# A third pair of k-tiles by seven products in the key and value blocks, and a softmax turned one unit later

## The chip, the cores and the metric

The kernel runs on one core of one Trainium2 chip. The core has a matrix engine (PE in the profile, with its weight loads as PEld), three engines for element work (DVE, which is VectorE; ACT, ScalarE; POOL, GpSimd) and SP, whose queue issues most DMAs. The metric is the device time of one execution in microseconds. Before the change it is 2083.93 us, the median of three runs from 2083.45 to 2084.53.

## The reference

One layer of a streaming encoder on 256 frames of width 2048, in float32: half a SwiGLU block, a mixer (pooling and gated linear attention), cross-attention to 256 memory tokens, half a SwiGLU block again, and a last norm. The change lies in the cross-attention:

```
def mem_cross_attention(h, mem_h, w_q, w_kv, w_o):
    q = (h @ w_q).reshape(b, s, XATTN_HEADS, XATTN_HEAD_DIM)
    kv = (mem_h @ w_kv).reshape(b, mem_h.shape[1], 2, XATTN_HEADS, XATTN_HEAD_DIM)
    k, v = kv[:, :, 0], kv[:, :, 1]
    logits = jnp.einsum('bshd,bmhd->bhsm', q, k).astype(jnp.float32) * (XATTN_HEAD_DIM ** -0.5)
    p = jax.nn.softmax(logits, axis=-1).astype(v.dtype)
    o = jnp.einsum('bhsm,bmhd->bshd', p, v).reshape(b, s, D_MODEL)
    return o @ w_o
```

There are 4 heads of width 512; `w_kv` is 2048 x 4096, keys first, values behind.

## The kernel before

**Split products.** A float32 matrix is kept as a high and a low part in the matrix engine's format, and a product is three matmuls: high by high, high by low, low by high. A weight that is loaded raw is therefore split: ACT casts the high part, DVE subtracts it from the raw tile for the low part.

**Units and blocks.** Weights come in units of 1 MB: 256 rows (a pair of k-tiles, numbered g = 0 to 7) by 1024 columns. A block is eight units that add into the same 256 x 1024 result. `Stream` (L34) emits the units in order. Before it emits unit u's matmuls it emits the splits of the units up to u + 2, and behind each split the load of the unit three further on. `st.op(f, n)` puts a function behind the n-th unit from there. The chains `in_turn` (L257) and `among_weights` (L270) keep the weight splits and some sums in the written order on ACT and DVE; apart from that a planner orders each engine's instructions at compile time, by its own estimates, so that an instruction which is not ready lets a later one pass. At run time each engine works its list in order.

**Plain and seven.** A plain unit (`unit_p`, L556) is 2 k-tiles x 2 token halves x 2 column halves = 8 products, 24 matmuls with 512 columns. A unit of a pair that is named in the block's `Sums` is done by Strassen's scheme in Winograd's form (`unit_s`, L539; `seven`, L493): 7 products, 21 matmuls. For that, DVE and ACT also form sums of the weights (`split_seven`, L471: three additions into a tile `T`, a split of three quarters of the raw tile into `xh` and `xl`, and a split of `T` into `wh` and `wl`), and once for all blocks, sums of the activations (`Sums.make`, L413).

**PSUM.** It is handed out as four tiles of 128 x 1024 (`ptile`, L137; the pool with 4 buffers, L109). A block holds two of them for the products of its plain units from its first unit to its last (`open_whole`), and two more from its first seven unit on (`open_parts`). `combine` (L570) reads these last two out behind the last seven unit, and `join` (L584) adds what it made to the other two at the block's end. Everything else that the matrix engine writes in that time, such as transposes (`rows_turned`, `probs`), `logits` and `values`, takes its tile from the same four.

**Cross-attention.** Keys and values are four blocks in a row: keys of heads 0 and 1, their values, keys of heads 2 and 3, their values. They are called K0, V0, K1 and V1 here. Each had two seven units, g = 0 and g = 4, at the places 3 and 6 of the order (1, 5, 2, 0, 3, 6, 4, 7), places counted from 0. `turn_K` runs behind the first unit of a V block, `logits` (with the softmax) behind its second, `probs`, which transposes the softmax and splits it, behind its third, and `values` behind the first unit of the block that follows. The buffers are tight in one more way: in these blocks `xh` and `xl` come from one group `att` of two buffers, and `T` from the group `sg`, of which `combine` takes one too:

```
KV_HOMES = {"T": [("sg", D, 2)], "xh": [("att", 3 * NB, 2)], "xl": [("att", 3 * NB, 2)]}
```

Of the kernel before, what the change touches and what calls it, by code (L numbers as in the profile page):

```python
# [15 lines left out]
D = 2048  # L16
# [4 lines left out]
NB = 512  # L21
# [78 lines left out]
def build(ctx, tc, I, out):  # L100
    nc = tc.nc
    st = Stream()
# [34 lines left out]
    def ptile(name):  # L137
        return psum.tile([P, 2, NB], F32, tag="ps", name=name)
# [6 lines left out]
    def uid(s):  # L145
        cnt[0] += 1
        return f"{s}{cnt[0]}"
# [42 lines left out]
    xs = main.tile([P, KT, 2, S], F32R, tag="xs", name="xs")  # L190
# [79 lines left out]
    def among_weights(f):  # L270


        scalar, vector = behind_weights(f)
        latest["vector"] = vector
        if scalar is not None:
            latest["scalar"] = scalar
# [7 lines left out]
    def split(hi, lo, src):  # L284
        high = nc.scalar.copy(hi, src)
        return high, nc.vector.tensor_tensor(out=lo, in0=src, in1=f32(hi), op=ALU.subtract)
# [339 lines left out]
    def wload(dst, w, k0, n, n0, cols=NB):  # L626
        nc.sync.dma_start(
            dst, w[k0 * P : (k0 + n) * P, n0 : n0 + cols].rearrange("(k p) n -> p k n", p=P)
        )
# [9 lines left out]
    def wwide(w, n0, k0=0, nk=KT):  # L639

        def src(k):
            def load(raw):
                raw = raw.rearrange("p (k n) -> p k n", n=2 * NB)
                if len(loaded) < 3:
                    for kk in range(2):
                        parts = (0, NB) if not loaded else (0,)
                        for c in parts:
                            n = 2 * NB // len(parts)
                            wload(raw[:, kk : kk + 1, c : c + n], w, k + kk, 1, n0 + c, n)
                else:  # L650
                    wload(raw, w, k, 2, n0, 2 * NB)
                next(first_loads, None)
                loaded.append(1)
            return load
        return [src(k0 + k) for k in range(0, nk, 2)]
# [557 lines left out]
    for b in range(2):  # L1213
        block_b(wblock(w_in, (4 + b) * NB), xs, ev_v(b))
        for i in range(2):
            h = 2 * b + i
# [16 lines left out]
    def homes(of):  # L1233
        return lambda: scope.update(shared={tag: list(of[tag]) for tag in of})
# [7 lines left out]
    def xt(name, shape, dt=F32, tag=None, bufs=1):  # L1242
        t = whole_lines(scope["pool"], shape, dt, tag or name, uid(name), bufs)
        xa[name] = t
        return t
# [36 lines left out]
    w_q, w_kv, w_o = I["xattn_w_q"][0], I["xattn_w_kv"][0], I["xattn_w_o"][0]  # L1282
# [2 lines left out]
    q_sums, Q_ORDER = Sums("ye", xs, (4, 5), True, 2), ((0, 1, 2, 3, 6, 4, 5, 7),  # L1285
                                                        (0, 1, 4, 2, 5, 3, 6, 7))
    Q_SEVENS = ((4,), (4, 5))
    kv_sums, KV_ORDER = Sums("ye", xs, (0, 4), True, 2), (1, 5, 2, 0, 3, 6, 4, 7)
    held = {}

    def ev_Q(b):
# [10 lines left out]
    def turn_K(h):  # L1302
        v = rows_turned(held["K", h])
        K = xa["K", h] = xt("K", [P, 4, 2, M], F32R, tag="kv", bufs=2)
        split(K[:, :, 0, :], K[:, :, 1, :], v)

    def ev_V(b):
        def evict(j, c):
            V = xa["V", 2 * b + j] = xt("V", [P, 2, 2, XHD], F32R, tag="kv", bufs=2)
            split(V[:, :, 0, :], V[:, :, 1, :], c)  # L1310
        return evict

    def logits(h):
        ps = ptile(uid("pl"))
        for t in range(2):
            tok = slice(t * P, (t + 1) * P)
            parts = [(d, a, b) for d in range(4) for a, b in ((0, 0), (0, 1), (1, 0))]
            for i, (d, a, b) in enumerate(parts):
                nc.tensor.matmul(  # L1319
                    ps[:, t, :M], ys[:, 4 * h + d, a, tok], xa["K", h][:, d, b, :],  # L1320
                    start=i == 0, stop=i == 11,
                )
        scale = XHD ** -0.5
        nm, sm = xt("nm", [P, 2], bufs=2), xt("sm", [P, 2], bufs=2)
        nc.vector.tensor_reduce(out=nm, in_=ps[:, :, :M], axis=AX.X, op=ALU.max)
        nc.vector.tensor_scalar_mul(nm, nm, -scale)
        pr = xa["P", h] = xt("P", [P, 2, M], bufs=2)
        for t in range(2):
            nc.scalar.activation(
                pr[:, t, :], ps[:, t, :M], AF.Exp, scale=scale, bias=nm[:, t : t + 1],  # L1330
                accum_out=sm[:, t : t + 1],
            )
        nc.vector.reciprocal(out=sm, in_=sm)
        for t in range(2):
            nc.vector.tensor_scalar_mul(pr[:, t, :], pr[:, t, :], sm[:, t : t + 1])

    def probs(h):
        ps = ptile(uid("pt"))
        for mtile in range(2):
            for t in range(2):  # L1340
                nc.tensor.transpose(
                    ps[:, mtile, t * P : (t + 1) * P], xa["P", h][:, t, mtile * P : (mtile + 1) * P], ident
                )
        if h % 2 == 0:
            xt("PT", [P, D], F32R)
        PT = xa["PT", h] = xa["PT"][:, h % 2 * 4 * S : (h % 2 + 1) * 4 * S].rearrange(
            "p (m a s) -> p m a s", m=2, a=2
        )
        split(PT[:, :, 0, :], PT[:, :, 1, :], ps[:, :, :S])

    def values(h):
        for p in range(2):
            ps = ptile(uid("pv"))
            for d in range(2):
                col = slice((2 * p + d) * P, (2 * p + d + 1) * P)
                parts = [(m, a, b) for m in range(2) for a, b in ((0, 0), (0, 1), (1, 0))]
                for i, (m, a, b) in enumerate(parts):
                    nc.tensor.matmul(  # L1358
                        ps[:, d, :S], xa["V", h][:, m, a, col], xa["PT", h][:, m, b, :],
                        start=i == 0, stop=i == 5,  # L1360
                    )
            split_pair(ys, 4 * h + 2 * p, ps[:, :, :S])
# [8 lines left out]
            for c, after in enumerate((5, 7, 6, 9)):  # L1371
                st.op(lambda c=c: mem_fold(c), after)
    st.op(homes(KV_HOMES))
    for g, after in zip(kv_sums.pairs, (0, 2)):
        st.op(lambda g=g: among_weights(lambda: kv_sums.make(g)), after)
    for b in range(2):
        block_s(wwide(w_kv, b * 2 * NB), xs, kv_sums, KV_ORDER, lambda j, c, b=b: held.__setitem__(
            ("K", 2 * b + j), c))
        for j in (1, 0):
            h = 2 * b + j  # L1380
            st.op(lambda h=h: turn_K(h), 1)
        for h in (2 * b, 2 * b + 1):
            st.op(lambda h=h: logits(h), 2)
            st.op(lambda h=h: probs(h), 3)
        block_s(wwide(w_kv, D + b * 2 * NB), xs, kv_sums, KV_ORDER, ev_V(b))
        for h in (2 * b, 2 * b + 1):
            st.op(lambda h=h: values(h), 1)
    st.op(homes(OUT_HOMES))
# [203 lines left out]
def program(shapes):  # L1592
    import concourse.bacc as _bacc

    nc = _bacc.Bacc("TRN2", target_bir_lowering=False, num_devices=1)
    args = {
        name: nc.dram_tensor(f"in_{name}", shapes[name], F32, kind="ExternalInput").ap()
        for name in _INS
    }
    out = nc.dram_tensor("out", _OUT, F32, kind="ExternalOutput").ap()  # L1600
    with tile.TileContext(nc, schedule_with_timeline_sim=True) as tc, ExitStack() as ctx:
        build(ctx, tc, args, out)
    return nc
# [10 lines left out]
```

## Time and profile before

| what | number |
| --- | --- |
| median of the runs | 2083.93 us |
| profiled execution, its whole time | 2082.87 us |
| its span (first to last instruction) | 2081.1 us |
| PE busy | 2069.4 us, 9660 matmuls |
| DVE busy | 1786.8 us |
| ACT busy | 1138.7 us |
| share of the 16 DMA engines in the loads' queue | 61.8% |
| granted clock of the matrix engine | 0.999 |
| block K0 | about 1089.8 to 1134.6 us of the span |
| block V0 | about 1134.6 to 1185.4 us |
| block K1 | about 1185.4 to 1233.3 us |
| block V1 | about 1233.3 to 1284.0 us |

In the profile's rows, L362 are the matmuls of `products`, so plain units; L507 those of `seven`. Where a short instruction of one kind stands amid another, the planner has interleaved units. A row of the timeline has the start in us, the duration in us, the engine, the line and the operation, the tile written and the tiles read, and in square brackets the engine's idle time ahead and what ended it. A mean duration of a matmul is longer than its share of the engine's time, since matmuls overlap: the pace is read from long runs of them. The program splits the weights of a plain unit at L1572 (ACT) and L453 (DVE); those of a seven unit at L486 (sums), L279 and L280 (`xh`, `xl`), L489 and L453 (`T`). On a block's last units POOL takes 768 of the 2048 columns of L453 (L457).

### The profile page before, as it was taken

To read this page: it belongs to the slowest core of one execution; us is meant where nothing else is said; L and a number is where in the kernel's file an instruction comes from. 1 tells how busy PE (TensorE), PEld (TensorE's weight loads), DVE (VectorE), ACT (ScalarE), POOL (GpSimd) and SP (SyncE) were. 2 spreads that over 40 slices of the span, in tenths; PEclk is the share of its full clock that TensorE was granted. 3 is DMA by queue.
4 is the path that set the end of the run, shared out by engine and by line. 5 is a ranking of instruction groups with operands and counts; after the bars stand their busy time and mean duration, and the time that the engine had idled before them with its cause. 6 is when DMAs were issued, how large, how long until landed. Compare 5 with 4: busy or idle time off the path is not lost.

```text
span 2081.1 us, 24346 instructions
## 1 busy us (share of the span) xinstructions
PE 2069.4 (99%) x9660; PEld 1727.4 (83%) x9660; DVE 1786.8 (86%) x1670; ACT 1138.7 (55%) x1128; POOL 98.4 (5%) x87
## 2 busy tenths in 40 slices
PE   9999999999999999999999999999999999999998
PEld 7888888888888888888888888888888888888886
DVE  7998899989998677679788777879988999889987
ACT  7655455644654545455755444656554555545554
POOL 0000000000000000000000000000100010000001
PEclk9999999999999999999999999999999999999999
DMA  7666666566656755557655455666576665676664
GB/s 264 208 199 228 234 223 220 184 222 240 225 200 218 249 166 182 162 185 272 227 179 189 161 182 181 204 222 204 181 243 215 234 209 191 224 242 222 211 226 150
DMA packets 131322, 435.95 MB, mean 209 GB/s; under 512 B 9860, under 2 KB 13544, under 8 KB 130824
## 3 DMA queue, kind: packets, MB, share of 16 engines
q1 hardware_dynamic: 131176, 434.38, 61.8%
q8 instruction: 76, 1.25, 0.2%
q14 instruction: 38, 0.31, 0.0%
q10 hardware_dynamic: 32, 0.01, 0.0%
HBM read 417.58 MB, written 16.78 MB: 209 GB/s over the span
## 4 chain that ended last, share of the span: by engine, by line
PE 99%; DMA 0%; DVE 0%; ACT 0%; SPq 0%; DVEq 0%; issue 0%; ACTq 0%
PE pt L362 59%; PE pt L507 27%; PE pa L347 7%; PE pb L362 2%; PE ph L780 1%; PE pl L1319 1%; PE pv L1358 1%; PE px L791 1%; PE pp L1012 0%; PE pe L362 0%; DMA x<-in_x 0%; PE pa L1039 0%; PE po L1161 0%; PE tm L1267 0%; PE px L717 0%; PE pq L1148 0%
## 5 line engine op out<-in xcount | busy, mean ns | idle before, releaser
L362 PE MATMUL pt<-wh,xs 128*128 128x512 f32 x2128 | 682.4, 390 | 0.3 <-ACT xs L236 0.3
L453 DVE TENSOR_TENSOR wl<-raw,wh 128x2048 fp32r<-128x2048 f32 (+1 forms) x256 | 552.3, 2163 | 141.5 <-ACT wh L1572 141.1
L1572 ACT CAST wh<-raw 128x2048 fp32r<-128x2048 f32 x256 | 489.4, 1913 | 299.9 <-PE pt L362 138.4
L362 PEld LDWEIGHTS pt<-wh,xs 128*128 128x128 f32 x2128 | 398.7, 188 | 82.1 <-ACT xs L236 0.6
L362 PE MATMUL pt<-wh,ys 128*128 128x512 f32 x1472 | 463.8, 389 | 0.0
L489 ACT CAST wh<-T 128x1024 fp32r<-128x1024 f32 x236 | 248.1, 1055 | 363.8 <-DVE T L486 355.4
L362 PE MATMUL pt<-wl,xs 128*128 128x512 f32 x1064 | 414.6, 390 | 0.0
L362 PEld LDWEIGHTS pt<-wh,ys 128*128 128x128 f32 x1472 | 276.2, 188 | 56.9
L362 PE MATMUL pt<-wl,ys 128*128 128x512 f32 x736 | 286.8, 390 | 0.0
L453 DVE TENSOR_TENSOR wl<-T,wh 128x2048 fp32r<-128x2048 f32 (+1 forms) x118 | 264.8, 2244 | 0.8 <-ACT wh L489 0.4
L362 PEld LDWEIGHTS pt<-wl,xs 128*128 128x128 f32 x1064 | 199.8, 188 | 41.0 <-DVE wl L280 0.2
L280 DVE TENSOR_TENSOR xl<-raw,xh 128x1536 fp32r<-128x1536 f32 x118 | 206.7, 1752 | 18.9 <-ACT xh L279 18.9
L279 ACT CAST xh<-raw 128x1536 fp32r<-128x1536 f32 x118 | 174.6, 1479 | 45.1 <-PE pt L507 36.3
L486 DVE TENSOR_TENSOR T<-T,raw 128x512 f32<-128x512 f32 x236 | 163.0, 691 | 6.2
L362 PEld LDWEIGHTS pt<-wl,ys 128*128 128x128 f32 x736 | 138.2, 188 | 28.5
L486 DVE TENSOR_TENSOR T<-raw 128x1024 f32<-128x1024 f32 x118 | 143.9, 1220 | 0.5
L507 PE MATMUL pt<-wh,xs 128*128 128x512 f32 x364 | 141.8, 390 | 0.0
L457 POOL TENSOR_TENSOR wl<-raw,wh 128x768 fp32r<-128x768 f32 x40 | 74.0, 1851 | 1376.2 <-DVE wl L453 1351.4
L507 PE MATMUL pt<-xh,xs 128*128 128x512 f32 x364 | 135.8, 389 | 0.0
L347 PE MATMUL pa<-xs,wh 128*128 128x512 f32 x384 | 135.6, 397 | 0.0
L507 PE MATMUL pt<-wh,xe 128*128 128x512 f32 x320 | 124.3, 389 | 0.0
L347 PE MATMUL pa<-xs,wl 128*128 128x256 f32 x384 | 106.8, 282 | 0.0
(248 smaller groups left out, 2312.2 us busy)
## 6 DMA issues: line engine op xcount, KB each, us to landing
raw<-in_ffn_w_down SPq DMA_DIRECT2D x88, 1024.0 KB, 5.5
raw<-in_ffn_w_up SPq DMA_DIRECT2D x80, 1024.0 KB, 5.0
raw<-in_ffn_w_gate SPq DMA_DIRECT2D x77, 1024.0 KB, 5.1
raw<-in_w_in SPq DMA_DIRECT2D x32, 1024.0 KB, 5.2
raw<-in_xattn_w_kv SPq DMA_DIRECT2D x32, 1024.0 KB, 5.0
raw<-in_w_out SPq DMA_DIRECT2D x16, 1024.0 KB, 5.6
raw<-in_xattn_w_q SPq DMA_DIRECT2D x16, 1024.0 KB, 5.5
raw<-in_xattn_w_o SPq DMA_DIRECT2D x16, 1024.0 KB, 5.6
```

Source lines behind the costliest of these rows:

```text
L279: in_turn("scalar", lambda: nc.scalar.copy(hi, src))
L280: in_turn("vector", lambda: nc.vector.tensor_tensor(out=lo, in0=src, in1=f32(hi), op=ALU.subtract))
L347: nc.tensor.matmul(o, w, x, start=k == 0 and i == 0, stop=last and i == 1)
L362: nc.tensor.matmul(ps, a, w, start=first and i == 0, stop=last and i == 2)
L453: in_turn("vector", lambda: nc.vector.tensor_tensor(out=lo[:, :n], in0=src[:, :n], in1=f32(hi[:, :n]), op=ALU.subtract))
L457: rest = nc.gpsimd.tensor_tensor(out=lo[:, n:], in0=src[:, n:], in1=f32(hi[:, n:]), op=ALU.subtract)
L486: in_turn("vector", lambda: nc.vector.tensor_tensor(out=o, in0=a, in1=b, op=ALU.add))
L489: in_turn("scalar", lambda: nc.scalar.copy(th[:, c], t[:, c]))
L507: nc.tensor.matmul(banks[n], x, w, start=n in fresh and j == 0, stop=n in ends and j == 2)
L780: nc.tensor.transpose(v[:, i, h * P : (h + 1) * P], g[:, h, i * P : (i + 1) * P], ident)
L791: nc.tensor.transpose(v[:, j, h * P : (h + 1) * P], x[:, h, j * P : (j + 1) * P], ident)
L1572: in_turn("scalar", lambda: nc.scalar.copy(hi, raw))
```

## The change

The key and value blocks take a third pair, g = 2, by seven products. K0 gets an order of its own with the seven units at the places 3, 5 and 6; in V0, K1 and V1 they stand at the places 1, 4 and 6. The activations' sums of the new pair are formed behind the third unit of K0, and the tile that holds such sums grows from two pairs to three. `probs` moves from behind the third unit of a V block to behind its fourth.

```
-    kv_sums, KV_ORDER = Sums("ye", xs, (0, 4), True, 2), (1, 5, 2, 0, 3, 6, 4, 7)
+    kv_sums = Sums("ye", xs, (0, 4, 2), True, 3)
+    KV_ORDER = ((1, 5, 3, 0, 6, 4, 2, 7), (1, 0, 3, 5, 2, 6, 4, 7))
...
-    for g, after in zip(kv_sums.pairs, (0, 2)):
+    for g, after in zip(kv_sums.pairs, (0, 2, 3)):
         st.op(lambda g=g: among_weights(lambda: kv_sums.make(g)), after)
     for b in range(2):
-        block_s(wwide(w_kv, b * 2 * NB), xs, kv_sums, KV_ORDER, lambda j, c, b=b: held.__setitem__(
+        block_s(wwide(w_kv, b * 2 * NB), xs, kv_sums, KV_ORDER[b], lambda j, c, b=b: held.__setitem__(
             ("K", 2 * b + j), c))
...
         for h in (2 * b, 2 * b + 1):
             st.op(lambda h=h: logits(h), 2)
-            st.op(lambda h=h: probs(h), 3)
-        block_s(wwide(w_kv, D + b * 2 * NB), xs, kv_sums, KV_ORDER, ev_V(b))
+            st.op(lambda h=h: probs(h), 4)
+        block_s(wwide(w_kv, D + b * 2 * NB), xs, kv_sums, KV_ORDER[1], ev_V(b))
```

## The prediction

> **What bounds the kernel now.** I read the page first, then the list of waits, then the chain, and last the timelines of the engines between 1060 and 1310 us, where keys and values are computed.
>
> ```profile
> PE 2069.4 (99%) x9660; PEld 1727.4 (83%) x9660; DVE 1786.8 (86%) x1670; ACT 1138.7 (55%) x1128; POOL 98.4 (5%) x87
> PE 99%; DMA 0%; DVE 0%; ACT 0%; SPq 0%; DVEq 0%; issue 0%; ACTq 0%
> 1124.61 4.76 PE pt L507 x21
> 1129.37 10.89 PE pt L362 x48
> 1066.35 0.19 PEld L507 LDWEIGHTS pt<-xl,xs 128*128 128x128 f32 x1 [0.39 <-DVE xl L280]
> 1068.26 0.19 PEld L362 LDWEIGHTS pt<-wh,xs 128*128 128x128 f32 x1 [0.21 <-ACT wh L1572]
> 1068.84 0.19 PEld L507 LDWEIGHTS pt<-wl,xs 128*128 128x128 f32 x1 [0.39 <-DVE wl L453]
> ```
>
> The matrix engine is busy for 99% of the span and carries 99% of the chain that ended last, so the time falls when matmuls go and rises when it has to wait. The next two lines, of the chain, give its pace: 10.89 / 48 = 0.227 us for a matmul of 512 columns, 5.44 us for a plain unit, and 4.76 us for a seven unit. The last three are the only waits of the matrix engine in the whole stretch, 0.99 us, and they lie in the query block, where two seven units with one plain unit between them ran late. In K0, V0, K1 and V1 it waits for nothing. These windows show what room DVE has there (the rows are K0, V0, K1, V1 and, for comparison, a block of the first stage of the last FFN; after the length come busy time and count of PE, PEld, DVE, ACT, POOL):
>
> ```profile
> 1089.80:1134.60 44.80, 44.80 (x211) 37.42 (x210) 39.43 (x45) 25.83 (x27) 2.95 (x2) 1.00 0.56 188
> 1134.60:1185.40 50.80, 50.80 (x260) 43.19 (x260) 36.04 (x35) 24.72 (x26) 3.27 (x3) 1.00 0.49 165
> 1185.40:1233.30 47.90, 47.90 (x235) 40.62 (x234) 34.21 (x28) 22.89 (x19) 3.63 (x3) 1.00 0.52 177
> 1233.30:1284.00 50.70, 50.70 (x259) 43.15 (x259) 36.38 (x36) 23.66 (x25) 3.71 (x3) 1.00 0.49 167
> 1661.80:1702.60 40.80, 40.80 (x182) 33.80 (x181) 39.04 (x30) 24.08 (x21) 2.57 (x2) 1.00 0.63 209
> ```
>
> DVE is 71 to 72% busy in V0, K1 and V1 and 88% in K0; the FFN runs at 96% without a wait. ACT, POOL and the DMAs (0.49 to 0.56 of their time) are far from full.
>
> **The matmuls that go.** Four units, one in each block, drop from 24 to 21 matmuls: 12 x 0.227 = 2.72 us. The Trainium skill ("TensorE: Matmul & The Clock Gate", Back-to-back issue gap) gives N/2.4 + 2.5 ns, so 216 ns for 512 columns, for an isolated stream; by it the saving would be an estimated 2.59 us. The measured 227 ns decides.
>
> **What the sums cost DVE.** Rows of a seven unit, of a plain unit (the fifth), and of the activations' sums:
>
> ```profile
> 1114.50 1.22 DVE L486 TENSOR_TENSOR T<-raw 128x1024 f32<-128x1024 f32 x1
> 1116.30 1.41 DVE L486 TENSOR_TENSOR T<-T,raw 128x512 f32<-128x512 f32 x2
> 1117.63 1.75 DVE L280 TENSOR_TENSOR xl<-raw,xh 128x1536 fp32r<-128x1536 f32 x1
> 1119.30 2.29 DVE L453 TENSOR_TENSOR wl<-T,wh 128x2048 fp32r<-128x2048 f32 x1
> 1121.51 2.29 DVE L453 TENSOR_TENSOR wl<-raw,wh 128x2048 fp32r<-128x2048 f32 x1
> 1106.17 0.68 DVE L424 TENSOR_TENSOR j<-xs 128x512 f32<-128x512 f32 x1
> 1109.88 0.29 DVE L436 TENSOR_TENSOR j<-j 128x128 f32<-128x128 f32 x1
> 1115.63 0.28 DVE L286 TENSOR_TENSOR xs<-j,xs 128x128 fp32r<-128x128 f32 x1
> 1115.84 0.55 DVE L286 TENSOR_TENSOR ye<-j,ye 128x384 fp32r<-128x384 f32 x1
> 1126.63 1.49 DVE L453 TENSOR_TENSOR wl<-raw,wh 128x1280 fp32r<-128x1280 f32 x1 [2.84 <-ACT wh L1572]
> ```
>
> A seven unit costs DVE 1.22 + 1.41 + 1.75 + 2.29 = 6.67 us against 2.29, so 4.38 us more per block. In V0, K1 and V1 this fits (36.38 + 4.38 of some 50 us). The new activations' sums, once in K0, are 0.68 + 4 x 0.29 + 0.28 + 0.55 = 2.67 us. K0's DVE then has 39.43 + 4.38 + 2.67 = 46.5 us of work in 44.1. What covers the missing 2.4 us is its lead: it stood idle for 2.84 us late in K0 because the three weight buffers were full. I take zero for this; without that lead it costs 2.4 us.
>
> In K0 the seven units at the places 5 and 6 touch. `xh` and `xl` share two buffers, so the second unit's cast waits until the first has done its nine products with them, 9 x 0.227 = 2.0 us in; then come the cast, `xl` (1.75) and `wl` (2.29), some 7.6 us in with the cast's 1.48 (row below), while the second unit starts at 4.76. High-part matmuls and the plain unit behind can fill part. I take the nearest row, the query block's 0.99 us; bounds: 0 (all filled) and 1.9 us (nothing reordered). In the other blocks at least one plain unit (5.44 us) lies between, which covers it.
>
> **Where the softmax finds no PSUM.** The blocks' order decides this. Rows around V0 (three of a window table of L507 alone, then the timelines):
>
> ```profile
> 1158.50:1161.00 2.50, 2.24 (x9) 1.53 (x9) 1.00 0.00 0
> 1161.00:1169.00 8.00, 0.21 (x1) 0.00 (x0) 1.00 0.39 132
> 1169.00:1172.20 3.20, 2.88 (x12) 2.25 (x12) 1.00 0.02 5
> 1160.38 0.60 PE L1341 MATMUL pt<-ident,P 128*128 128x128 f32 x4
> 1162.91 0.60 PE L1341 MATMUL pt<-ident,P 128*128 128x128 f32 x4
> 1164.59 1.28 DVE L286 TENSOR_TENSOR PT<-pt,PT 128x512 fp32r<-128x512 f32 x2
> 1169.92 1.48 ACT L279 CAST xh<-raw 128x1536 fp32r<-128x1536 f32 x1 [5.79 <-PE pt L507]
> ```
>
> The first seven unit of V0 does its nine matmuls for the two old PSUM tiles at 1158.5 (the 1 in the second row is its ninth, running over), and the twelve for the two new ones only at 1169, after the softmax transposes (L1341) and their reads at 1164.59. The tiles are handed out in the written order, and a tile promised to the softmax is not lent out. The matrix engine lost nothing, since plain units filled in, but the next `xh` came 5.79 us late.
>
> With the first seven unit at place 1, the order is reversed: it takes the two free tiles behind `turn_K`, and `logits` has to wait until `combine` gives them back at the block's end. The softmax then meets the block's end, where DVE has this to do:
>
> ```profile
> 1180.52 0.69 DVE L575 TENSOR_TENSOR sg<-pt,sg 128x512 f32<-128x512 f32 x1 [1.29 <-ACT sg L574]
> 1181.24 1.23 DVE L576 TENSOR_TENSOR sg<-pt,sg 128x1024 f32<-128x1024 f32 x1
> 1182.51 0.69 DVE L579 TENSOR_TENSOR sg<-pt,sg 128x512 f32<-128x512 f32 x1
> 1183.11 1.49 DVE L453 TENSOR_TENSOR wl<-raw,wh 128x1280 fp32r<-128x1280 f32 x1
> 1184.51 2.35 DVE L589 TENSOR_TENSOR sg<-pt,sg 128x1024 f32<-128x1024 f32 x2
> 1150.57 5.63 PE pl L1319 x47
> 1153.37 0.69 DVE L1325 TENSOR_REDUCE nm<-pl 128x2 f32<-128x512 f32 x1 [1.56 <-PE pl L1319]
> 1154.34 1.28 ACT L1329 ACT_TABLE_LOAD   x1 [4.86 <-DVE nm L1326]
> 1156.45 0.20 ACT L1329 ACTIVATION_READ_ACCUMULATOR P<-pl,nm 128x1 f32 x1
> 1156.89 0.62 DVE L1335 TENSOR_SCALAR P<-P,sm 128x256 f32<-128x256 f32 x2
> ```
>
> Count from the start of `combine`. The matrix engine has the last plain unit until 5.1 and the logits of two heads (5.63 x 48/47 = 5.75 us) until 10.8. After that it can go on only with transposes of a ready softmax, or with the next block, which needs two PSUM tiles. DVE: `combine` until 2.7; then, for K1, the seven unit at place 1, 1.22 + 1.41 + 1.75 + 1.49 = 5.9, until 8.6; the first head's maximum until 9.4; one `join` until 10.6; the other until 11.8. The first head's PSUM tile is read out at about 11.7 (2.3 us behind the maximum, for the table load and the exponentials, 1154.34 to 1156.65). The softmax transposes come first in the written order and take the first two tiles that come free, so the next block gets the third, freed at 11.8; I take 12.3, as the scaling of the first head (0.62) stands among the joins on DVE: **V0 to K1 costs 1.5 us**. Bounds: 0, if the planner hands the block an earlier tile; 4.3, if it puts the second head's transposes ahead of the block (logits end at 10.8, and from the maximum to the scaled softmax pass 1157.5 - 1153.4 = 4.1 us). At V1's end the unit behind is plain, 1.49 in place of 5.9, the joins are done by 7, and the next block waits for the first head's tile alone, at about 11.4: **0.6 us**, bounds 0 and 3.6.
>
> The move of `probs` by one unit adds nothing: eight transposes and two casts, later than `logits` in any case; what needs them is `values`, behind the first unit of the next block. V's splits and `values` slide back by as much as the softmax; K1's plain units at the places 2 and 3 (10.9 us) cover that, and without them the waits of the row [5.79 <-PE] would reach the matrix engine. The loads on SP are as many, in another order, each behind its split; POOL's 768 columns now belong to the sum tile three times, at equal size. I put both at nothing, under DMA shares of about a half.
>
> On PSUM the Trainium skill ("Perfetto Trace Analysis", Optimization Strategy) says that a gap which keeps repeating on the engine that should be saturated can mean too little SBUF or PSUM for the next tile. The trace of before has no such gap in these blocks; by that rule one would appear at both ends of the V blocks.
>
> **The sum.** -2.72 + 0.99 + 1.5 + 0.6 = +0.4 us, so 2082.87 (profiled execution: span 2081.1 and 1.77 around it) becomes 2083.3. The median stands 1.06 above that execution, which gives **2084.3 us**. With all waits at their lower ends it is 2083.93 - 2.72 = 2081.2; with all at their upper ends and the 2.4 us of K0, +12.2 - 2.72 = 2093.4. Re-planning could also remove the query block's 0.99 us; more cannot be gained.
>
> **The rivals.**
> - *All cover holds.* Plain units fill K0's end and the block gets its tiles early: 2081.2 us. For it: no wait in four blocks now, and the planner moved twelve matmuls by 8 us unharmed. Against it: at a V block's end no plain unit is left to move.
> - *The softmax's second head bars the way* (the slower side). At both V ends the planner sets both heads' transposes ahead of the next block: 4.3 + 3.6 + 0.99 = 8.9 of waits, 2083.93 - 2.72 + 8.9 = 2090.1. It decides against the change once both V ends together cost more than 2.72 - 0.99 = 1.73 us, and by over 0.2% from 5.9 us on. For it: the written order, and tiles kept for the softmax at 1161 to 1165. Against it: PE could take the block's unit first.
> - *DVE becomes the bound in K0*: 2.4 us more, 2086.7. For it: 46.5 us in 44.1; against it: the FFN at 96% without a wait.
> - *The sums don't reach all four blocks*: they share one `kv_sums`, so 12 matmuls must go. I give this no chance of its own.
>
> **The chances.** Forecast 0.50 (own range 2081.9 to 2088), all cover holds 0.22, second head bars 0.20, DVE in K0 0.06, other 0.02. About 0.2% (4.2 us) is what a measurement of this kernel can tell from no change, so from 2079.8 to 2088.1 counts as the same. The saving cannot reach the lower bound: faster 0.02. Slower: the second head's case and a little of the others, 0.22. The same: 0.76. The range runs from 2081.0 to 2090.5, from all cover to just past the second head's case.
>
> **What would show it.** In the changed trace: 9648 matmuls; L1319 no longer amid the V blocks but after their last L507; an idle matrix engine, released by DVE (L589) or ACT (L1329), ahead of the first unit of K1, and a smaller one ahead of the output block; a short wait for `xl` or `wl` late in K0. Wrong would be: logits still behind the second unit, so that the seven unit's tiles came later; or waits inside the blocks, where I see cover.

## The result, and the profile after

The changed kernel takes 2100.38 us (median of five runs, 2099.73 to 2100.94), the kernel before 2083.78 us beside it (2083.45 to 2084.53). The ratio is 1.0079, with a 95% interval from 1.0068 to 1.0091: slower by 16.6 us. The forecast was 2084.3 us, the range ended at 2090.5, and the time lies outside it.

From the page of the changed kernel, the span, the busy times, and the chain by engine; then, from its list of waits of the matrix engine (engine, waiting group, releaser, then us in total, times, longest), the first row:

```profile
span 2098.2 us, 24353 instructions
PE 2073.4 (99%) x9648; PEld 1728.0 (82%) x9648; DVE 1804.8 (86%) x1693; ACT 1146.9 (55%) x1138; POOL 98.4 (5%) x87
PE 96%; DVE 2%; DMA 0%; ACT 0%; issue 0%; SPq 0%; DVEq 0%; ACTq 0%
```

```profile
PE pt L1342 <- DVE P L1336: 12.1, 3, 6.4
```

The twelve matmuls are gone (9648 against 9660), yet PE is busy for 4.0 us longer, and DVE now stands in the chain. One wait that was not there before takes 12.1 us: the transposes of the softmax (L1342; L1341 before) wait for its scaled rows. The length of each block, from its first matmul to the first matmul of the block behind it, and the same for the experiments told of below (OUT is the first block of the output projection):

| kernel | K0 | V0 | K1 | V1 | OUT |
| --- | --- | --- | --- | --- | --- |
| before | 44.85 | 50.72 | 47.98 | 50.70 | 47.97 |
| after | 46.26 | 56.88 | 49.85 | 56.07 | 50.09 |
| e1 `probs` behind the next unit | 46.32 | 49.03 | 49.32 | 49.03 | 49.07 |
| e2 `probs` back | 46.31 | 57.00 | 49.39 | 56.06 | 49.82 |
| e3 `logits` a unit earlier | 46.32 | 55.26 | 49.95 | 51.29 | 48.08 |
| e4 the V order alone | 44.85 | 61.45 | 49.82 | 55.67 | 50.02 |
| e5 third pair in K0 alone | 46.18 | 50.72 | 47.98 | 50.70 | 47.97 |
| e6 third pair in K1 alone | 44.85 | 50.72 | 50.41 | 50.70 | 47.97 |
| e7 V blocks in K0's order | 46.25 | 54.84 | 49.74 | 50.57 | 48.12 |
| e8 three blocks of four | 44.85 | 49.02 | 49.32 | 49.03 | 49.02 |
| e9 K0's two units touching | 47.14 | 50.72 | 47.98 | 50.70 | 47.97 |
| e10 K0's three units spread | 46.72 | 50.71 | 47.98 | 50.70 | 47.97 |
| e11 V blocks alone | 44.85 | 49.03 | 49.34 | 49.68 | 49.10 |

After against before: +1.41, +6.16, +1.87, +5.37 and +2.12, which with 0.14 ahead of K0 is 17.1 us, the difference of the two spans. Most of it lies at the ends of V0 and V1. The timeline of the matrix engine there, in the changed kernel:

```profile
1179.46 5.91 PE L1320 MATMUL pl<-K,ys 128*128 128x256 f32 x48
1191.78 1.63 PE L1342 MATMUL pt<-ident,P 128*128 128x128 f32 x5 [6.41 <-DVE P L1336]
1193.07 0.78 PE L362 MATMUL pt<-wh,xs 128*128 128x512 f32 x1
...
1198.93 0.49 PE L1342 MATMUL pt<-ident,P 128*128 128x128 f32 x3
...
1286.20 5.91 PE L1320 MATMUL pl<-K,ys 128*128 128x256 f32 x48
1296.90 1.08 PE L1342 MATMUL pt<-ident,P 128*128 128x128 f32 x4 [4.79 <-DVE P L1336]
1298.88 0.45 PE L1342 MATMUL pt<-ident,P 128*128 128x128 f32 x1 [0.90 <-DVE P L1336]
1298.99 0.78 PE L362 MATMUL pt<-wh,ys 128*128 128x512 f32 x1
...
1304.83 0.49 PE L1342 MATMUL pt<-ident,P 128*128 128x128 f32 x3
```

The logits of both heads stand behind the block's last unit, as forecast, and end at 1185.4. Then PE does nothing for 6.41 us at V0's end and for 4.79 + 0.90 us at V1's. At both ends all four transposes of the first head and one of the second run ahead of the next block, and the other three follow later. When PE resumes, it does so slowly: from 1193.07 to 1198.93 it gets through 18 matmuls of K1's first unit, 326 ns each on average in place of 227, and from 1298.99 to 1304.83 through 18 of the output block's. The window table over the first of these stretches has the reason in the granted clock, the number behind the busy times and counts of the five engines:

```profile
1185.40:1189.00 3.60, 0.00 (x0) 0.00 (x0) 3.60 (x4) 2.33 (x3) 0.00 (x0) 1.00 0.20 83
...
1189.50:1195.50 6.00, 3.62 (x11) 2.78 (x12) 3.84 (x11) 2.63 (x9) 0.00 (x0) 0.53 0.46 166
1195.50:1196.00 0.50, 0.50 (x3) 0.40 (x2) 0.00 (x0) 0.00 (x0) 0.00 (x0) 0.50 0.00 0
1196.00:1200.00 4.00, 4.00 (x19) 3.23 (x19) 0.00 (x0) 0.54 (x1) 0.00 (x0) 0.92 0.00 0
```

The clock falls to half amid the idle stretch and stays there until about 1196.6. Before, it was 1.00 in all these blocks. Half clock costs 5.86 - 18 x 0.227 = 1.8 us in K1 and as much in OUT, the largest part of what these two lost (+2.12 in OUT; +1.87 in K1, where three matmuls, 0.68 us, are gone as well). The busy PE of the page hides it, since a slow matmul is a busy one.

What DVE did in that time (timeline of DVE, changed kernel, and one row of ACT, the end of the first head's exponentials):

```profile
1183.02 2.35 DVE L589 TENSOR_TENSOR sg<-pt,sg 128x1024 f32<-128x1024 f32 x2
1185.29 0.68 DVE L1326 TENSOR_REDUCE nm<-pl 128x2 f32<-128x512 f32 x1
1185.88 2.28 DVE L453 TENSOR_TENSOR wl<-raw,wh 128x2048 fp32r<-128x2048 f32 x1
1188.08 0.68 DVE L1326 TENSOR_REDUCE nm<-pl 128x2 f32<-128x512 f32 x1
1188.68 1.22 DVE L286 TENSOR_TENSOR V<-sg,V 128x1024 fp32r<-128x1024 f32 x1
1189.82 0.16 DVE L1327 TENSOR_SCALAR nm<-nm 128x2 f32<-128x2 f32 x1
1189.88 1.22 DVE L286 TENSOR_TENSOR V<-sg,V 128x1024 fp32r<-128x1024 f32 x1
1191.02 0.16 DVE L1327 TENSOR_SCALAR nm<-nm 128x2 f32<-128x2 f32 x1
...
1191.28 0.62 DVE L1336 TENSOR_SCALAR P<-P,sm 128x256 f32<-128x256 f32 x2
```

```profile
1190.83 0.20 ACT L1330 ACTIVATION_READ_ACCUMULATOR P<-pl,nm 128x1 f32 x1
```

Both `join`s (L589) are over at 1185.4, so the block's two tiles are free then, together with the logits' end. The next block does not get them. It starts only behind the first transposes. The softmax itself is slow: from its first maximum at 1185.29 to the first head's scaled rows at 1191.9 it takes 6.6 us, and a plain unit's split (2.28), the second head's maximum (0.68) and the splits of V (1.22 each) stand between its small steps on DVE.

### The profile page after: what moved, and what is told of

It reads as the page before. It is cut to its first block, busy times and chain, and to the rows that moved or that the text cites. A ratio compares the mean times of both kernels' runs of the same rounds, so it can differ in the third digit from the quotient of the medians.

```text
span 2098.2 us, 24353 instructions
## 1 busy us (share of the span) xinstructions
PE 2073.4 (99%) x9648; PEld 1728.0 (82%) x9648; DVE 1804.8 (86%) x1693; ACT 1146.9 (55%) x1138; POOL 98.4 (5%) x87
## 3 DMA queue, kind: packets, MB, share of 16 engines
q8 instruction: 76, 1.25, 0.2%
## 4 chain that ended last, share of the span: by engine, by line
PE 96%; DVE 2%; DMA 0%; ACT 0%; issue 0%; SPq 0%; DVEq 0%; ACTq 0%
PE pt L362 56%; PE pt L507 27%; PE pa L347 6%; PE pb L362 2%; PE ph L780 1%; DVE wl L453 1%; PE pv L1359 1%; PE px L791 0%; DVE T L486 0%; DVE xl L280 0%; PE pp L1012 0%; PE pe L362 0%; DMA x<-in_x 0%; DMA raw<-in_xattn_w_kv 0%; DVE V L286 0%
## 5 line engine op out<-in xcount | busy, mean ns | idle before, releaser
L362 PE MATMUL pt<-wh,xs 128*128 128x512 f32 x2064 | 665.2, 391 | 0.1
L453 DVE TENSOR_TENSOR wl<-raw,wh 128x2048 fp32r<-128x2048 f32 (+1 forms) x252 | 545.3, 2170 | 130.3 <-ACT wh L1573 130.0
L1573 ACT CAST wh<-raw 128x2048 fp32r<-128x2048 f32 x252 | 481.6, 1913 | 277.2 <-PE pt L362 119.7
L489 ACT CAST wh<-T 128x1024 fp32r<-128x1024 f32 x244 | 256.4, 1054 | 374.7 <-DVE T L486 368.4
L362 PEld LDWEIGHTS pt<-wh,xs 128*128 128x128 f32 x2064 | 387.7, 188 | 80.4 <-ACT wh L1573 0.5
L362 PE MATMUL pt<-wl,xs 128*128 128x512 f32 x1032 | 402.8, 391 | 0.0
L453 DVE TENSOR_TENSOR wl<-T,wh 128x2048 fp32r<-128x2048 f32 (+1 forms) x122 | 271.5, 2225 | 0.8 <-ACT wh L489 0.4
L280 DVE TENSOR_TENSOR xl<-raw,xh 128x1536 fp32r<-128x1536 f32 x122 | 213.7, 1752 | 19.6 <-ACT xh L279 19.6
L279 ACT CAST xh<-raw 128x1536 fp32r<-128x1536 f32 x122 | 180.5, 1480 | 56.4 <-PE pt L507 42.6
L507 PE MATMUL pt<-wh,xs 128*128 128x512 f32 x380 | 147.9, 389 | 0.0
L507 PE MATMUL pt<-xh,xs 128*128 128x512 f32 x380 | 142.0, 389 | 0.0
```

Source lines behind the costliest of these rows:

```text
L279: in_turn("scalar", lambda: nc.scalar.copy(hi, src))
L280: in_turn("vector", lambda: nc.vector.tensor_tensor(out=lo, in0=src, in1=f32(hi), op=ALU.subtract))
L362: nc.tensor.matmul(ps, a, w, start=first and i == 0, stop=last and i == 2)
L453: in_turn("vector", lambda: nc.vector.tensor_tensor(out=lo[:, :n], in0=src[:, :n], in1=f32(hi[:, :n]), op=ALU.subtract))
L489: in_turn("scalar", lambda: nc.scalar.copy(th[:, c], t[:, c]))
L507: nc.tensor.matmul(banks[n], x, w, start=n in fresh and j == 0, stop=n in ends and j == 2)
```

## The experiments

Three theories of the V ends were set against each other. **A**: the transposes of both heads come before the next block in the written order, take the first tiles that come free, and bar the block. **B**: DVE has too much to do at the block's end with the third pair's splits, and would be late in any order of tiles. **C**: the move of `probs` by a unit is what hurts. For K0, a pair D and E came later, told with its two runs.

### e1: `probs` behind the first unit of the next block

```
-            st.op(lambda h=h: probs(h), 4)
+            st.op(lambda h=h: probs(h), 9)
```

> Only the place of probs changes against the changed kernel: from behind the fourth unit of a V block to behind the first unit of the next block, so that the next block's two PSUM tiles are written down ahead of the softmax transposes. Theory A (the tiles promised to the transposes bar the next block): the waits of 6.4 us ahead of the transposes L1342 go, and with them the half-clock stretches; 2083 to 2087 us. Theory B (DVE is too full at the V block's end, whatever the order): the next block still waits for DVE; 2096 to 2101 us.

Measured: 2084.26 us, ratio 1.0004 (0.9994 to 1.0013). V0 and V1 take 49.03 us. The timeline of its matrix engine and, in the second fence, of its DVE, at V0's end:

```profile
1179.84 5.92 PE L1320 MATMUL pl<-K,ys 128*128 128x256 f32 x48
1185.60 0.40 PE L362 MATMUL pt<-wh,xs 128*128 128x512 f32 x1
```

```profile
1183.38 2.35 DVE L589 TENSOR_TENSOR sg<-pt,sg 128x1024 f32<-128x1024 f32 x2
1185.64 0.68 DVE L1326 TENSOR_REDUCE nm<-pl 128x2 f32<-128x512 f32 x1
1186.24 2.28 DVE L453 TENSOR_TENSOR wl<-raw,wh 128x2048 fp32r<-128x2048 f32 x1
1188.44 0.68 DVE L1326 TENSOR_REDUCE nm<-pl 128x2 f32<-128x512 f32 x1
...
1191.65 0.62 DVE L1336 TENSOR_SCALAR P<-P,sm 128x256 f32<-128x256 f32 x2
```

DVE's list is the same and as late: the rows are scaled at 1191.65. But the block follows the logits at once, at 1185.60. So B falls as the account of this wait, and A is shown for it: DVE is as late, and the block does not need it. The semaphores in the two traces fit this: the first matmul of K1 waits on ACT in the changed kernel, which reads out the tiles of the logits, and on DVE in e1, which ran the `join`s. So only in e1 did the block get the joined tiles. The gain against the changed kernel, 15.6 us against the common before, is as much as the 12.1 us of waits and the 3.5 us of half clock together, although the moved transposes take a part back in K1 and OUT (K1 is only 0.53 us shorter than in the changed kernel).

### e2: `probs` back where it was

```
-            st.op(lambda h=h: probs(h), 4)
+            st.op(lambda h=h: probs(h), 3)
```

> Only probs goes back to where it was before, behind the third unit of a V block; the rest is the changed kernel. Theory A: logits are barred until combine in any case, so nothing moves; 2099 to 2102 us. Theory C (turning the softmax a unit later is what cost the time): most of the loss goes; 2084 to 2088 us.

Measured: 2099.72 us, ratio 1.0078 (1.0063 to 1.0093); the wait is 12.2 us, in place of 12.1. C falls: in this order of the units the move by a unit costs and brings nothing. The transposes wait for `logits`, which wait for tiles.

### e3: `logits` a unit earlier

```
-            st.op(lambda h=h: logits(h), 2)
+            st.op(lambda h=h: logits(h), 1)
```

> Only logits moves against the changed kernel, one unit up, so that its PSUM tiles are written down ahead of those of the seven unit at place 1. probs stays. Theory A: the softmax is done in the middle of the V block, only the transposes are left for the block's end, and the wait of 6.4 us shrinks below 1 us at both ends; 2084 to 2089 us. Theory B: the seven unit's sums, the joins and V's splits are still at the block's end on DVE, so at least half of the loss stays; 2092 us or more.

Measured: 2092.58 us, ratio 1.0041 (1.0027 to 1.0055), so better than the change, but beyond what A gave it and where B had put it. The logits now get the two tiles ahead of the seven unit at place 1. V1 nearly recovers (51.29 us), V0 does not (55.26). Its list of waits, the first row:

```profile
PE pt L362 <- DVE PT L286: 3.3, 1, 3.3
```

At V0's end the next block now stands behind the transposes' tiles themselves: they were done, and it waited until DVE had split what they wrote. The tile that the softmax holds is late again, at another of its steps. The timeline of DVE shows why it was late (two rows):

```profile
1190.16 1.75 DVE L280 TENSOR_TENSOR xl<-raw,xh 128x1536 fp32r<-128x1536 f32 x1
1191.82 1.28 DVE L286 TENSOR_TENSOR PT<-pt,PT 128x512 fp32r<-128x512 f32 x2
```

The transposes end at 1189.25, but DVE is at the sums and at `xl` of K1's own seven unit at place 1, and comes to them only at 1191.82. The output block has no seven unit so early, and V1's end does not wait. So A's mechanism, tiles promised in written order, remains; its reading that only the place of `logits` mattered does not, and B is right in part: once a tile is promised to the softmax, DVE's other work decides how late it comes free.

### e4: the V order alone, without the third pair

```
-    kv_sums = Sums("ye", xs, (0, 4, 2), True, 3)
-    KV_ORDER = ((1, 5, 3, 0, 6, 4, 2, 7), (1, 0, 3, 5, 2, 6, 4, 7))
+    kv_sums = Sums("ye", xs, (0, 4), True, 2)
+    KV_ORDER = ((1, 5, 2, 0, 3, 6, 4, 7), (1, 0, 3, 5, 2, 6, 4, 7))
...
-        block_s(wwide(w_kv, b * 2 * NB), xs, kv_sums, KV_ORDER[b], lambda j, c, b=b: held.__setitem__(
+        block_s(wwide(w_kv, b * 2 * NB), xs, kv_sums, KV_ORDER[0], lambda j, c, b=b: held.__setitem__(
```

K0 and K1 are as before, V0 and V1 have two seven units, at the places 1 and 6; all matmuls of before are there.

> No third pair at all: the kernel before, with only the order of the V blocks changed to that of the changed kernel (seven units at the places 1 and 6, two in each block) and probs behind the fourth unit. DVE has no more work than before. Theory A: logits are barred as in the changed kernel and the V ends cost the same, some 17 us in all without the 2 us of K0; 2096 to 2102 us. Theory B: without the additional sums on DVE it costs little; 2083 to 2088 us.

Measured: 2103.99 us, ratio 1.0097 (1.0082 to 1.0112), slower than the change itself and than expected. Rows of its matrix engine at V0's end:

```profile
1186.17 0.72 PE L1342 MATMUL pt<-ident,P 128*128 128x128 f32 x4 [1.09 <-DVE P L1336]
1196.56 0.45 PE L1342 MATMUL pt<-ident,P 128*128 128x128 f32 x1 [9.67 <-DVE P L1336]
```

The first head is ready at 1186.17, and the second holds the block up for 9.67 us more. So moving the first seven unit to place 1 (with `probs` behind the fourth unit) is enough for the loss, and neither the third pair nor DVE's work for it is needed.

### e7: the V blocks in K0's order

```
-        block_s(wwide(w_kv, D + b * 2 * NB), xs, kv_sums, KV_ORDER[1], ev_V(b))
+        block_s(wwide(w_kv, D + b * 2 * NB), xs, kv_sums, KV_ORDER[0], ev_V(b))
```

> The changed kernel, but V0 and V1 in K0's order (seven units at the places 3, 5, 6), so that logits find two free PSUM tiles ahead of the first seven unit, as in the kernel before. probs stays behind the fourth unit, so behind that first seven unit. Theory A: the long waits at the V ends go for the logits, but the transposes are still written behind the seven unit's tiles and in front of the next block, which costs 3 to 4 us at an end, and the touching seven units cost some 2 us in each of K0, V0, V1; 2090 to 2097 us. Rival (only the logits' place matters): 2084 to 2088 us.

Measured: 2091.61 us, ratio 1.0040 (1.0025 to 1.0056), within what was expected, although the loss was expected at both ends. V1 is as short as before (50.57 us), V0 is not (54.84), and its waits are headed by

```profile
PE pt L362 <- DVE PT L286: 4.1, 1, 4.1
```

Even with the first seven unit back at place 3, V0's end waits, as in e3, for the split of what the transposes wrote, and K1, which still has its seven unit at place 1, again puts that unit's sums ahead of it on DVE. So K0's order in the V blocks is not a cure by itself; `probs` behind the next block's first unit (e1) is one. Whether K0's order with `probs` back behind the third unit would be another, as in the kernel before, was not run.

### e5 and e6: the third pair in one K block alone

The pair g = 2 gets sums in a tile of its own, so that the other blocks can take it as a plain unit. Common to e5, e6, e8, e10 and e11:

```
-                t = scope["pool"].tile([P, room * 6 * P], F32R, tag=tag, name=uid(tag))
+                t = scope["pool"].tile([P, max(6 * room, 2 * n) * P], F32R, tag=tag, name=uid(tag))
...
-    kv_sums = Sums("ye", xs, (0, 4, 2), True, 3)
+    kv_two, kv_one = Sums("ye", xs, (0, 4), True, 2), Sums("yf", xs, (2,), False, 1)
+
+    class KvSums:
+        pairs = (0, 4, 2)
+
+        def make(self, g):
+            return (kv_one if g == 2 else kv_two).make(g)
+
+        def parts(self, g):
+            return (kv_one if g == 2 else kv_two).parts(g)
+
+    kv_sums = KvSums()
```

e5 leaves K0 as changed and gives K1, V0 and V1 the old order, `sevens=(0, 4)`, and `probs` the old place; e6 does the same with K1 in place of K0, and forms the pair's sums behind the fourteenth unit:

```
-    for g, after in zip(kv_sums.pairs, (0, 2, 3)):
+    for g, after in zip(kv_sums.pairs, (0, 2, 14)):
```

> The third pair by seven in K0 alone, in the changed kernel's order (places 3, 5, 6); V0, K1, V1 and probs as in the kernel before (the new pair's sums are kept in a tile of their own, so that the other blocks can take the pair plainly). Theory A: the waits late in K0 that the changed trace shows (0.4 + 0.5 + 1.4 + 0.3 = 2.6 us) outweigh the 0.68 us of three matmuls; +1 to +2 us on the kernel before. Rival: they are paid back later in the block; -0.7 us.

> The third pair by seven in K1 alone, at the places 1, 4 and 6; all else as in the kernel before. No logits in K1, so no PSUM tile is barred by the seven unit at place 1 but those of values. Theory A: the saving stands by itself, -0.7 us, or 0 where values' four tiles delay the seven unit at place 1. Rival (DVE is too full for a seven unit between combine and join): +1 us or more.

Measured: e5 2084.52 us, ratio 1.0007 (0.9999 to 1.0016); e6 2085.56 us, ratio 1.0012 (1.0003 to 1.0020). The times hardly differ from before, the blocks do: K0 is 1.33 us longer and K1 2.43 us, with three matmuls fewer in each. For K1 a gain of up to 0.7 us was expected of theory A, and it was missed: the 2.3 us by which e6 is slower lie with the rival (DVE too full, +1 us or more). Two rows of e6's matrix engine early in K1:

```profile
1194.13 0.50 PE L507 MATMUL pt<-wl,xs 128*128 128x512 f32 x1 [0.46 <-POOL wl L457]
1196.03 0.74 PE L1370 MATMUL pv<-PT,V 128*128 128x256 f32 x4 [0.93 <-ACT V L285]
```

The seven unit at place 1 puts its sums and splits on DVE and ACT in between the end of V0 and the splits of V, and both the unit and `values` come late. This is read from the trace, and it is not the third pair's weights alone: the pair's activation sums, formed behind the fourteenth unit, end on DVE only at 1184.57, in the middle of `combine` and 1.7 us ahead of K1's first matmul. e6 does not tell the two apart.

### e9 and e10: why K0 waits

In the changed kernel's K0 four weight loads wait, 2.61 us in all, where 0.99 was forecast (timeline of the weight loads, then a window of the 28 us in which they lie):

```profile
1120.14 0.19 PEld L507 LDWEIGHTS pt<-xl,xs 128*128 128x128 f32 x1 [0.36 <-DVE xl L280]
1122.34 0.19 PEld L507 LDWEIGHTS pt<-wl,xs 128*128 128x128 f32 x1 [0.52 <-DVE wl L453]
1126.60 0.19 PEld L507 LDWEIGHTS pt<-xl,xs 128*128 128x128 f32 x1 [1.44 <-DVE xl L280]
1128.80 0.19 PEld L507 LDWEIGHTS pt<-wl,xs 128*128 128x128 f32 x1 [0.29 <-DVE wl L453]
```

```profile
1108.00:1136.20 28.20, 27.09 (x117) 21.29 (x116) 27.66 (x32) 14.52 (x15) 1.85 (x1) 1.00 0.51 161
```

DVE is busy for 27.66 of 28.2 us, which speaks against the buffers that the prediction blamed. The cast of the last seven unit and its `xl` say the same (timelines of ACT and DVE):

```profile
1121.65 1.48 ACT L279 CAST xh<-raw 128x1536 fp32r<-128x1536 f32 x1 [2.14 <-PE pt L507]
1124.80 1.75 DVE L280 TENSOR_TENSOR xl<-raw,xh 128x1536 fp32r<-128x1536 f32 x1
```

The cast did wait 2.14 us for a buffer and ended at 1123.13, but DVE, without a pause, came to its `xl` only at 1124.80. So e9 keeps before's work and lets the two seven units touch (in the kernel before, `KV_ORDER if b else (1, 5, 3, 2, 6, 0, 4, 7)` for the K blocks), and e10 keeps e5's work and lets none touch (the sums ahead of the first unit, behind the first and behind the third; the expectation counts one unit more each time):

```
-    KV_ORDER = ((1, 5, 3, 0, 6, 4, 2, 7), (1, 0, 3, 5, 2, 6, 4, 7))
+    KV_ORDER = ((1, 5, 0, 3, 4, 6, 2, 7), (1, 0, 3, 5, 2, 6, 4, 7))
...
-    for g, after in zip(kv_sums.pairs, (0, 2, 3)):
+    for g, after in zip(kv_sums.pairs, (0, 1, 3)):
```

> The kernel before, with its two seven units of K0 put next to each other, at the places 5 and 6; nothing else differs, so DVE has no more work in K0 than before. It asks why the changed K0 waits 2.6 us. Theory D (DVE is the bound in K0: it runs without a pause from 1108 us on, and the third pair's sums and splits are what it is late with): without that work the touching units cost at most 0.5 us, K0 stays within 44.8 to 45.4 us. Theory E (the two buffers of xh and xl, as the prediction had it: the second of two touching units gets its cast late, whatever DVE has to do): waits for xl and wl of 1.0 to 2.6 us remain, K0 takes 45.8 to 47.4 us.

> The third pair in K0 alone, as in the run that had it there, but with the three seven units at the places 2, 4 and 6, a plain unit between any two, and the activations' sums behind the first, second and fourth unit. Theory D: DVE has the same 6.9 us more to do in K0 as in that run; the waits move but stay at 1.5 us or more in sum, K0 takes 45.5 us or more. Theory E: no two units touch, so the waits go and K0 takes 44.85 - 0.68 = 44.2 us, give or take 0.3.

Measured: e9 2085.41 us, ratio 1.0011 (1.0002 to 1.0020), K0 47.14 us; e10 2085.13 us, ratio 1.0010 (1.0001 to 1.0019), K0 46.72 us. The timelines of DVE and of ACT in e9, one row each from around the second unit's cast, and of the weight loads in e10, those that wait:

```profile
1125.21 1.76 DVE L280 TENSOR_TENSOR xl<-raw,xh 128x1536 fp32r<-128x1536 f32 x1 [7.70 <-ACT xh L279]
```

```profile
1123.70 1.48 ACT L279 CAST xh<-raw 128x1536 fp32r<-128x1536 f32 x1 [11.55 <-PE pt L507]
```

```profile
1107.60 0.19 PEld L507 LDWEIGHTS pt<-xh,xs 128*128 128x128 f32 x1 [0.62 <-ACT xh L279]
1110.53 0.19 PEld L362 LDWEIGHTS pt<-wl,xs 128*128 128x128 f32 x1 [1.47 <-DVE wl L453]
1121.44 0.19 PEld L362 LDWEIGHTS pt<-wl,xs 128*128 128x128 f32 x1 [0.83 <-DVE wl L453]
```

Each theory is right where it was set alone, and neither excludes the other. In e9 DVE and ACT stand idle for 7.70 and 11.55 us until PE has given a buffer back, and K0 loses 2.29 us: E. In e10 no units touch, DVE is busy for 45.29 of 46.7 us, and plain units wait for their low parts; K0 loses 1.87 us and the 0.68 saved: D. The changed K0 has both conditions, but its rows show DVE as the one that came last; the buffers cost it nothing that can be seen. With less work on DVE they could be next, so that a cure may need a third buffer too; that was not run.

### e8 and e11: what is left of the gain

e8 gives the third pair to V0, K1 and V1, K0 staying as before, with `probs` behind the next block's first unit as in e1, and forms the pair's sums behind the sixth unit. e11 does so for V0 and V1 alone (K1 with the old order and `sevens=(0, 4)`):

```
-    for g, after in zip(kv_sums.pairs, (0, 2, 3)):
+    for g, after in zip(kv_sums.pairs, (0, 2, 6)):
...
-            st.op(lambda h=h: probs(h), 4)
+            st.op(lambda h=h: probs(h), 9)
```

> An attempt to keep the gain: K0 as in the kernel before (two seven units), V0, K1 and V1 with three at the places 1, 4 and 6, probs behind the first unit of the next block. Nine matmuls fewer, 2.04 us. Theory A: neither of the two losses is left, so 1 to 2 us under the kernel before. Rival (the crowded block ends still cost): no gain, 0 to +2 us.

> The third pair in V0 and V1 alone, at the places 1, 4 and 6, with the softmax's transposes behind the first unit of the block that follows; K0 and K1 as before with two seven units. Six matmuls fewer than before, 1.36 us. If the V blocks lose nothing inside, as the blocks of the run with three of four suggest, and the 1 us that K1 lost there came from K1's own third seven unit: 2081.9 us, 1.4 below before. If K1 loses it to the later transposes and values instead: 2083, no difference from before. Neither is far enough from before for the times alone; the lengths of K1 (47.98 us before, 49.32 with three seven units and the moved transposes) tell: 49.0 or less for the first, 49.9 for the second.

Measured: e8 2082.61 us, ratio 0.9996 (0.9988 to 1.0005); e11 2083.45 us, ratio 1.0001 (0.9992 to 1.0010). Neither can be told from before. By blocks, e8 saves 1.70 and 1.67 us in V0 and V1 and gives 1.34 and 1.05 back in K1 and OUT, a net 0.98 of the 9 x 0.227 = 2.04 us that its matmuls are worth. A V block's gain would be 0.68 us of matmuls, and the other 1.0 us goes with the transposes, which only moved to the next block; OUT, which has no third pair, is longer by as much (1.05). The rest of the loss lies in K1: with the third pair it is 1.34 us longer than before, where the moved transposes less the saved matmuls would make it 0.3. Five weight loads of K1 wait there, 1.47 us in all, 1.25 us of it for DVE. In e11, without that pair in K1, K1 takes 49.34 us, between the two values expected, and three weight loads wait 0.72 us, so that neither answer is right alone; V1 lost another 0.65 us there, in one wait of 0.63 us for a plain unit's low part. No version beat the kernel before by more than the measurement can tell.

## Why the prediction was wrong

**What bounds the kernel** was right: PE sets the pace, and all that was lost is time in which it waited or ran at half clock.

**The matmuls that go**: 12, as counted. No run shows their 0.68 us a block by itself: the V blocks of e1 and e8 are 1.7 us shorter, with the transposes gone from them as well.

**What the sums cost DVE in K0** was forecast as 0.99 us, for the buffers, with bounds from 0 to 1.9, and DVE's own shortage of 2.4 us was taken as zero. The weight loads waited 2.61 us, a part of which the matmuls in front of them covered; K0 is 1.41 us longer with 0.68 us of matmuls fewer, so it lost 2.09 us, close to the term that was put at nothing. DVE's lead did not cover it. The rival "DVE becomes the bound in K0" was right in its place, and its chance of 0.06 too small.

**Where the softmax finds no PSUM** is the step that failed, by its choice and by its size. The mechanism was seen: the logits at the block's end, the tiles promised to the softmax, an idle engine there. The Trainium skill's sentence on repeating gaps ("Perfetto Trace Analysis", Optimization Strategy) pointed to both ends of the V blocks, and the gap is there; but two of the four tiles were free throughout it, so that the fault was not too little PSUM but whom the tiles were promised to. The forecast let the next block start as soon as the third tile was read out, that of the first head's logits (1.5 and 0.6 us), and put "the softmax's second head bars the way" at 0.20. What happened is nearly the second, at both ends: the block came behind the first head's four transposes and the first of the second head's. V1's end shows it best (timeline of ACT, the end of the first head's exponentials):

```profile
1291.29 0.20 ACT L1330 ACTIVATION_READ_ACCUMULATOR P<-pl,nm 128x1 f32 x1
```

The third tile was read out at 1291.49, ahead of the logits' end at 1292.1 and earlier than forecast, and yet the output block started only at 1298.99. So the idle engine was released by the scaled rows (L1336), and not by L589 or L1329 as the prediction had it. The price was too low too, in three ways:
- The waits were 6.41 us in place of the upper bound of 4.3, and 4.79 + 0.90 in place of 3.6. The bound of 4.3 rests on 4.1 us from the maximum to the scaled softmax, from a stretch in which DVE had time for it; for 3.6, and for the 1.9 in K0, the prediction shows no working. At V0's end the same steps took 6.6 us, with 2.28 + 2 x 1.22 = 4.7 us of splits in between, and at V1's 7.75. The count had put a seven unit's sums ahead of the softmax and the two `join`s into it. But both `join`s came ahead of the first maximum, and the splits came between the steps, so that V0's first exponentials ended 16.3 us behind the start of `combine` (1174.77), where 11.7 was forecast.
- V1's end was held to be cheap, as a plain unit follows there. It was nearly as dear: the output block's activation sums, a plain split and V's splits stand there in its place.
- The half clock behind each wait, 3.5 us in sum, was not in the sum at all.

With 12.1 + 3.5 of these, 2.09 in K0, and 2.72 saved, 15.0 of the 17.1 us are accounted for. The rest lies in part with transposes that ran at half clock (four in 1.08 us at 1296.90, where four took 0.60 before), and perhaps with K1's splits; it was not divided further.

**The move of `probs`** adds nothing: right in the changed order (e2). What the text missed is that a larger move, past the first unit of the next block, takes the whole loss at the V ends away (e1).

**The interior of the V blocks**: no wait appeared there, right.

## What to carry to other kernels

When a schedule hands out buffers in written order, look at whom the next tile is promised to, and not only at whether one is free: in this case two free tiles stood unused for 6 us because a slower consumer was written first, and one number in one line gave 15.6 us back. When a wait is priced by a duration, take that duration from a stretch in which the engine is as loaded as it will be, with its other work in between. And a saving of 0.7 us a block asks for the engines beside it to have slack at the same place: here DVE, ACT and the transposes' place took half of it back in the best version (e8), and nearly all of it or more in the others.

## What the runs showed of the hardware

A wait of the matrix engine of some 3.3 us or more cost more than its length. After 6.41 and 4.79 us without matmuls its clock stood at one half, each time for some 6.8 us (1189.9 to 1196.6 by the windows above, and 1295.6 to 1302.5), part of it in the idle stretch and the rest in matmuls. After the 3.31 us wait of e3 it was one half too, for a shorter time (some 3.4 us), and after the 4.1 us of e7 for no longer than that; window table of e3:

```profile
1191.50:1192.50 1.00, 0.00 (x0) 0.00 (x0) 1.00 (x3) 1.00 (x2) 0.00 (x0) 1.00 0.00 0
1193.50:1195.00 1.50, 1.50 (x5) 1.14 (x4) 1.50 (x2) 0.16 (x1) 0.33 (x1) 0.50 0.82 287
1195.00:1197.00 2.00, 2.00 (x8) 1.61 (x7) 2.00 (x3) 1.24 (x2) 1.51 (x1) 0.75 0.67 274
1197.00:1200.00 3.00, 3.00 (x15) 2.46 (x14) 3.00 (x2) 0.86 (x1) 0.00 (x0) 1.00 0.00 0
```

PE's waits of about 1 us in K0 and in e6 left the clock at 1.00. The Trainium skill ("TensorE: Matmul & The Clock Gate", Part 1) says that the clock falls to half after at least one idle window of some 3.4 us, and rises again after a busy one of that length; the runs agree with it, as far as waits of 3.31 us (a little under that window) and above against 1.0 us and below can tell.
